# A hybrid retention and attention layer on one core: the feed forward in three chunks, with the output shares of two chunks computed as seven block products instead of eight

## The chip, the cores and the metric

The kernel runs on one core of a Trainium2 chip. The metric is the time of one execution on the device, in microseconds (us). The core's engines are named as in the profile: PE (matrix products; PEld is its loading of weights), DVE (vector engine), ACT (scalar engine), POOL and SP. SP issues nearly all DMA transfers here. The kernel is one hand-ordered program: each engine takes its instructions in the order in which the Python code emits them.

## The reference

One inference step of a layer, for a prompt of 512 tokens and for 8 sample tokens that continue from stored state. D_MODEL is 1024, the hidden width of the feed forward 2816 (22 x 128); all is fp32.

```python
proj = rmsnorm(x, g1) @ w_in            # q,k,v,g of 4 retention heads; q,k,v of 12 attention heads; 2 gates
o_r, s_new = retention(rotary(q_r), rotary(k_r), v_r, state, chunk=128)
branch_a = (group_norm(o_r) * gn_g * silu(g_r)) @ w_pa
branch_b = combine(dilated_attention(q_a, k_a, v_a)) @ w_pb      # three groups of heads
h = x + (sigmoid(gate_a) * branch_a + sigmoid(gate_b) * branch_b) @ w_o
a, b = split(rmsnorm(h, g2) @ w_ffn_in)
h = h + (silu(a) * b) @ w_ffn_out
y = rmsnorm(h, g_final)
```

Outputs are y, the retention states and the new keys and values, for prompt and samples.

## The kernel before

**Layout.** Activations lie transposed: 128 channels on the partitions, and on the free axis C = 520 columns in two halves f of HF = 260 (256 prompt tokens and 4 samples each). All weights of all projections lie in one tensor `wall` of 194 pieces ("subs") of 128x1024, in the order in which they are needed; a sub holds eight 128x128 tiles. A projection's output tile (128 channels) sums over its k-tiles: 8 where the input has 1024 channels, 22 for `w_ffn_out`.

**Products.** An fp32 product is made of three products of a shorter type (fp32r): both operands are split in a high part and the remainder, and w x = wh xh + wh xl + wl xh (`product`). With two halves, one tile of weights costs six matmuls of 128x260. `unit` runs `nk` tiles of weights into one buffer `pm` (two PSUM banks, one per half) and then calls the evacuation given to it.

**The weights' way.** SP loads a sub into one of four buffers `raw` (`load_sub`). `split_sub` has ACT copy it to `wh` (L153) and DVE subtract to `wl` (L157). At each eighth tile `unit` has the sub after next split; the subtraction and the next load are held back by two pumps:

```python
A.activation(h, r, AF.Copy)                                       # L153: wh
    V.tensor_tensor(l, r, f32(h), op=ALU.subtract)                # L157: wl
    load_sub(s + NRAW)
later(2, low)
```

**The order of the work.** After each tile of weights `unit` calls `pump`, which first runs what `later(n, ...)` held back for n pumps, and then lets the generators in the tracks P, S and Q go one step. So everything beside the big products (norms, attention, retention, the sample states) is emitted in steps between the matmuls. `drain` runs a track to its end at one place.

**The stages.** Norm and `w_in` with the retention heads (four of them, up to about 450 us), the gates, `w_pa`, attention, `w_pb`, `w_o`, then the feed forward. In a retention head, a generator updates the states of the 8 samples, two tiles of 128x512 each: ACT makes `kv` (L510) from `vb`, a broadcast load of one row (L502); DVE updates the state `st` (L545), SP stores it and reloads the buffer; ACT (L521) and DVE (L526) make `y` from it, and after each four samples PE sums four `y` into the bank `oacc` (L555). All this shares ACT and DVE with the splits of the weights.

**The feed forward.** It runs over 22 hidden tiles, each two units of eight k-tiles (a and b; `ev_fa`, `ev_fb` scale them by the norm `rs2`, L1112 multiplies them, ACT and DVE split the product into `U[i]` and `U[22 + i]`). Then come eight output tiles, each a unit of 22 k-tiles that `ev_f` adds to the residual `hT`. The last one is done a half at a time.

**The final norm.** For each output tile c and half f a round follows: `fin_T` transposes 2 x 128 tokens and 4 samples (three matmuls, L212) into two of the three side banks; `fin_sq` sums squares on ACT (L1142, L1144); `fin_g` multiplies by the gain on DVE (L1148, L1150) and so frees the banks. `gen_final(c)` emits both rounds of a tile in steps of the track P, beside the matmuls of the next tile. `fin_out(f)` ends a half: squares of tile 7, reduction (L1169), 1/rms (POOL), gain of tile 7, scaling, and the stores.

Of the kernel before, what the change touches and what calls it, by code (L numbers as in the profile page):

```python
# [23 lines left out]
NSUB = 194  # L24
GAMMA = [1.0 - 2.0 ** (-5.0 - h) for h in range(RH)]
# [3 lines left out]
def tile_hybrid_layer(  # L29
# [108 lines left out]
    raw, split = {}, {}  # L138

    NRAW = 4  # L140

    def load_sub(s):
# [4 lines left out]
    def split_sub(s):  # L147
        if s >= NSUB or s in split:
            return
        r = raw.pop(s)  # L150
        h = wpool.tile([128, 1024], F32R, tag="wh", name=f"wh{s}")
        l = wpool.tile([128, 1024], F32R, tag="wl", name=f"wl{s}")
        A.activation(h, r, AF.Copy)  # L153
        split[s] = (h, l)

        def low():
            V.tensor_tensor(l, r, f32(h), op=ALU.subtract)  # L157
            load_sub(s + NRAW)

        later(2, low)  # L160

# [20 lines left out]
    def product(pm, n, k, nk, src, fs):  # L182
        h, l = split[n // 8]
        j = n % 8
        wh, wl = h[:, j * 128:(j + 1) * 128], l[:, j * 128:(j + 1) * 128]
        xh, xl = src(k)
        for w, x, first, last in ((wh, xh, k == 0, False), (wh, xl, False, False), (wl, xh, False, k == nk - 1)):
            for f in fs:
                PE.matmul(pm[:, f, :HF], w, x[:, f * HF:(f + 1) * HF], start=first, stop=last)  # L189

    def unit(nk, src, evac=None):
        pm = pmain.tile([128, 2, 512], F32, tag="pm", name="pm")
        for k in range(nk):
            n = pos[0]
            pos[0] += 1
            if n % 8 == 0:
                for s in range(3):
                    split_sub(n // 8 + s)
# [4 lines left out]
        return pm[:, :, :HF]  # L203

# [42 lines left out]
    for s in range(2):  # L247
        split[s] = tuple(wpool.tile([128, 1024], F32R, tag=t, name=f"{t}{s}") for t in ("wh", "wl"))

    def w_split(s, i):  # L250
        q = slice(512 * i, 512 * i + 512)
        (h, l), r = split[s], raw[s]
        A.activation(h[:, q], r[:, q], AF.Copy)
        V.tensor_tensor(l[:, q], r[:, q], f32(h[:, q]), op=ALU.subtract)
# [10 lines left out]
    for s in range(2):  # L265
        raw.pop(s)
        load_sub(NRAW + s)
# [73 lines left out]
    for h in range(RH):  # L341
# [245 lines left out]
        for which in ("q", "k"):  # L587
            e0, e1 = rot(which)
            if h == 0 and which == "q":
# [3 lines left out]
                for u, k in [(u, k) for k in range(4) for u in range(2)] + [(u, k) for u in range(2) for k in range(4, 8)]:  # L593
                    product(pms[u], 8 * u + k, k, 8, src, (0, 1))
                    if u and k == 4:
                        split_sub(2)
# [446 lines left out]
    fp = open_pool("fp", "right")  # L1043
    X2 = bpool.tile([128, 16, C], F32R, tag="bx", name="X2")
# [50 lines left out]
    U = [None] * (2 * NFF)  # L1095
    UA = bpool.tile([128, 16, C], F32R, tag="bg", name="UA")
    UB = fp.tile([128, 28, C], F32R, name="UB")
    for i in range(2 * NFF):
        U[i] = UA[:, i, :] if i < 16 else UB[:, i - 16, :]
    for i in range(NFF):  # L1100
# [8 lines left out]
        def ev_fb(pm, i=i, s=s):  # L1109
            t = ftmp("fb")  # L1110
            V.tensor_tensor(halves(t), pm, halves(rs2), op=ALU.mult)  # L1111
            V.tensor_tensor(t, t, s["a"], op=ALU.mult)  # L1112
            A.activation(U[i], t, AF.Copy)
            later(2, lambda: V.tensor_tensor(U[NFF + i], t, f32(U[i]), op=ALU.subtract))
# [3 lines left out]
        if i == 0:  # L1118
            drain("P")
            ev_fa(pa)  # L1120
            ev_fb(pb)

# [29 lines left out]
    def gen_final(c):  # L1152
        for _ in range(5):
            yield
        a = fin_T(c, 0)
        yield
        fin_sq(c, 0, *a)
        fin_g(c, 0, *a)
        yield
        yield  # L1160
        b = fin_T(c, 1)
        yield
        fin_sq(c, 1, *b)
        fin_g(c, 1, *b)

    def fin_out(f, sp, sp2):
        fin_sq(7, f, sp, sp2)
# [3 lines left out]
        fin_g(7, f, sp, sp2)  # L1171
# [13 lines left out]
    def usrc(k):  # L1185
        return U[k], U[NFF + k]

    def ev_f(pm, c, f=None):
        fs = slice(None) if f is None else slice(f, f + 1)
        h = halves(hT[:, c, :])[:, fs]  # L1190
        V.tensor_tensor(h, pm[:, fs], h, op=ALU.add)
# [6 lines left out]
    for s in range(base // 8, NSUB):  # L1198
        split_sub(s)
    for f in range(2):  # L1200
        pm = pmain.tile([128, 2, 512], F32, tag="pm", name="pm")
        for k in range(NFF):
            product(pm, base + k, k, NFF, usrc, (f,))
            if f == 0 and k % 2:
                pump()
            if f == 1 and k == 2:
                a = fin_T(7, 0)
            if f == 1 and k == 5:
                fin_out(0, *a)
        ev_f(pm[:, :, :HF], 7, f)  # L1210
    a = fin_T(7, 1)
    fin_out(1, *a)
# [42 lines left out]
def _layout(np, i):  # L1255
# [9 lines left out]
    for h in range(AH):  # L1265
        for g in range(3):
# [3 lines left out]
    ffo = [j for c in range(NFF) for j in (c, NFF + c)]  # L1270
    flat = np.concatenate([x.reshape(-1, 128, 128) for x in
                           (w_in[seq], _tiles(f["w_pa"][0]), w_in[seq2], _tiles(f["w_pb"][0]), _tiles(f["w_o"][0]), ff[ffo],
                            _tiles(f["w_ffn_out"][0]))])
# [25 lines left out]
```

## Time and profile before

| | |
|---|---|
| Time, three runs | 1330.41, 1331.48 and 1332.78 us; median 1331.48 |
| The profiled execution | 1332.56 us, of it 1330.8 from its first to its last instruction (the span) |
| Mean granted clock of PE | 0.991 of full speed |
| After the last matmul of the products (L189) | 9.5 us |
| Moved from and to memory | 155.70 MB read, 25.98 MB written |

In the profile a line such as "L189 PE MATMUL pm<-X,wh" is a group of instructions: line of the kernel, engine, operation, output and inputs by the program's names. Behind it stand shape and count, the summed busy time in us and the mean of one in ns, and then the idle time in front of them on that engine, with what ended most of it. In the list of waits a row names who waited, for whom, the sum in us, the number of waits and the longest. The chain of waits is the work that ended last, followed back. A row of the chain in order of time starts with the moment and the duration, both in us. A window's row gives for a stretch the busy time of PE, PEld, DVE, ACT and POOL with the number of instructions, then the granted clock, the share of time of the DMA engines, and GB/s. In a row of the DMA view three numbers stand for a queue that waits for a transfer (sum, count, longest).

### The profile page before, as it was taken

The page shows a single profiled execution, that of the slowest core. Times are in us where ns is not written, and L with a number is a line of the kernel's source. Part 1 is how long each engine was busy: PE and PEld are TensorE (multiplying, and loading weights), DVE is VectorE, ACT ScalarE, POOL GpSimd, SP SyncE. Part 2 cuts the span into 40 slices and gives each one's busy share as a digit, 9 for nine tenths or more (in the row PEclk, how much of TensorE's full clock was granted, in tenths as well). Part 3 has the DMA queues.
Part 4 walks back from the last instruction along what each step waited for, and adds up shares of the span by engine and source line. Part 5 has one row for each costly group of instructions (what it writes and reads, how often), then busy time and mean ns, then how long its engine had stood idle before and what let it go on. Part 6 is the DMA issues. An engine that isn't in the chain of part 4 may idle for free.

```text
span 1330.8 us, 25131 instructions
## 1 busy us (share of the span) xinstructions
PE 1304.4 (98%) x10681; PEld 1273.4 (96%) x10681; DVE 662.5 (50%) x1271; ACT 476.7 (36%) x828; POOL 83.0 (6%) x69
## 2 busy tenths in 40 slices
PE   8999999999989999999999999999999999999997
PEld 7899999898889999999999999899999999999997
DVE  7867536746655432233545454376444444443323
ACT  4554334534453421143434343233222222222222
POOL 3601001001002000000000000030000000000000
PEclk9999999999899999999999999999999999999999
DMA  6267235646475233435555455634223332333221
GB/s 216 84 227 231 89 114 206 228 129 230 157 255 189 80 96 95 135 115 160 156 159 164 134 171 175 217 104 136 82 94 96 96 90 86 95 112 96 80 64 66
DMA packets 89777, 183.33 MB, mean 138 GB/s; under 512 B 12024, under 2 KB 33944, under 8 KB 89664
## 3 DMA queue, kind: packets, MB, share of 16 engines
q1 hardware_dynamic: 88944, 180.64, 43.2%
q8 instruction: 84, 1.38, 0.4%
q10 hardware_dynamic: 720, 1.07, 0.2%
q14 instruction: 29, 0.24, 0.1%
HBM read 155.70 MB, written 25.98 MB: 137 GB/s over the span
## 4 chain that ended last, share of the span: by engine, by line
PE 89%; DVE 4%; DMA 3%; ACT 1%; issue 1%; POOL 1%; SPq 1%; POOLq 0%; DVEq 0%; ACTq 0%
PE pm L189 78%; PE sp L212 3%; PE sp L442 2%; DMA vb<-vd 2%; PE sp L460 2%; DVE wl L157 1%; PE sp L394 1%; PE sp L852 1%; PE sp L802 1%; PE oacc L555 1%; PE sacc L997 1%; PE sp L791 0%; ACT wh L153 0%; DMA xb<-xT 0%; DVE X L313 0%
## 5 line engine op out<-in xcount | busy, mean ns | idle before, releaser
L189 PE MATMUL pm<-X,wh 128*128 128x260 f32 x4608 | 756.6, 286 | 3.9 <-DVE X L244 3.6
L189 PEld LDWEIGHTS pm<-X,wh 128*128 128x128 f32 x4608 | 636.7, 189 | 19.3 <-issue 8.2
L189 PE MATMUL pm<-X,wl 128*128 128x260 f32 x2304 | 465.0, 283 | 0.0
L189 PEld LDWEIGHTS pm<-X,wl 128*128 128x128 f32 x2304 | 356.3, 189 | 0.1
L157 DVE TENSOR_TENSOR wl<-raw,wh 128x1024 fp32r<-128x1024 f32 x192 | 236.6, 1233 | 169.9 <-ACT wh L153 169.2
L153 ACT ACTIVATE wh<-raw 128x1024 fp32r<-128x1024 f32 x192 | 201.7, 1051 | 174.2 <-PE pm L189 169.0
L189 PE MATMUL pm<-UB,wh 128*128 128x260 f32 x448 | 85.3, 282 | 0.0
L189 PE MATMUL pm<-GA,wh 128*128 128x260 f32 x512 | 82.2, 283 | 0.0
L189 PEld LDWEIGHTS pm<-GA,wh 128*128 128x128 f32 x512 | 70.1, 188 | 0.0
L189 PEld LDWEIGHTS pm<-UB,wh 128*128 128x128 f32 x448 | 67.2, 188 | 0.0
L221 POOL TENSOR_TENSOR r<-v,cst 128x4 f32<-128x4 f32 (+4 forms) x14 | 18.4, 1313 | 609.9 <-DVE v L219 609.8
L189 PE MATMUL pm<-UA,wh 128*128 128x260 f32 x256 | 55.3, 287 | 0.0
L510 ACT ACTIVATE kv<-vb,ks 128x512 f32<-128x512 f32 x64 | 44.0, 715 | 29.8 <-DMA vb<-vd 29.8
L545 DVE SCALAR_TENSOR_TENSOR st<-st,kv 128x512 f32<-128x512 f32 x64 | 45.9, 733 | 16.7 <-ACT kv L510 16.7
L189 PE MATMUL pm<-UA,wl 128*128 128x260 f32 x256 | 54.2, 283 | 0.0
L189 PE MATMUL pm<-GA,wl 128*128 128x260 f32 x256 | 51.6, 283 | 0.0
L1106 ACT ACTIVATE fa<-fa 128x520 f32<-128x520 f32 x22 | 14.0, 638 | 78.4 <-DVE fa L1105 78.4
L189 PE MATMUL pm<-M,wh 128*128 128x260 f32 x256 | 41.1, 282 | 0.0
L189 PEld LDWEIGHTS pm<-UA,wh 128*128 128x128 f32 x256 | 40.4, 188 | 0.3
L189 PEld LDWEIGHTS pm<-UA,wl 128*128 128x128 f32 x256 | 40.5, 188 | 0.0
L189 PEld LDWEIGHTS pm<-GA,wl 128*128 128x128 f32 x256 | 39.6, 188 | 0.0
L1111 DVE TENSOR_TENSOR fb<-pm,rs 128x520 f32<-128x520 f32 x22 | 15.4, 700 | 46.2 <-PE pm L189 46.2
(245 smaller groups left out, 1309.7 us busy)
## 6 DMA issues: line engine op xcount, KB each, us to landing
raw<-wall SPq DMA_DIRECT2D x192, 512.0 KB
st<-state SPq DMA_DIRECT2D x64, 256.0 KB
out<-st SPq DMA_DIRECT2D x64, 256.0 KB
area<-ck SPq DMA_DIRECT2D x24, 512.0 KB
vb<-vd SPq DMA_DIRECT2D x32, 256.0 KB
area<-qd SPq DMA_DIRECT2D x12, 512.0 KB
cb<-cd SPq DMA_DIRECT2D x4, 768.0 KB
xr<-xT SPq DMA_DIRECT2D x8, 260.0 KB
```

The source lines that it names most:

```text
L153: A.activation(h, r, AF.Copy)
L157: V.tensor_tensor(l, r, f32(h), op=ALU.subtract)
L189: PE.matmul(pm[:, f, :HF], w, x[:, f * HF:(f + 1) * HF], start=first, stop=last)
L212: PE.transpose(out, in_, ident[:n, :n])
L221: G_.tensor_tensor(r[:rows, :ncol], v[:rows, :ncol], mhalf[:rows].to_broadcast([rows, ncol]), op=ALU.pow)
L394: PE.matmul(sp[:, :T - i0], x[:, dt, jb * 128:(jb + 1) * 128], y[:, dt, i0:], start=i == 0, stop=i == len(mm) - 1)
L442: PE.matmul(sp[:, i0:], v[x][:, jb, c * 128:(c + 1) * 128], scs[y][:, SCO[jb]:SCO[jb] + T - i0], start=jb == 0 and x == y, stop=jb == 3 an ...
L460: PE.matmul(sp, kt[x][:, jb, dt * 128:(dt + 1) * 128], v[y][:, jb, :], start=jb == 0 and x == y, stop=jb == 3 and x == 1)
L510: A.activation(kvs[i][:, :DV], vbs[b], AF.Copy, scale=ks[:, dt, b:b + 1])
L545: V.scalar_tensor_tensor(sts[i], sts[i], GAMMA[h], kvs.pop(i)[:, :DV], op0=ALU.mult, op1=ALU.add)
L1106: A.activation(t, t, AF.Silu)
L1111: V.tensor_tensor(halves(t), pm, halves(rs2), op=ALU.mult)
```

## The change

**Blocks of 512.** Weights are split in blocks of 512 columns instead of 1024. `wh` and `wl` have six buffers of 512 each, and `advance` keeps the copies five blocks ahead of the product that runs. A `raw` buffer is reloaded when its second half is subtracted.

**Three chunks.** The hidden tiles are cut in chunks of 8, 8 and 6. After each of the first two chunks (and one tile of the next) comes that chunk's share of all eight output tiles, added to `hT`. The hidden tiles of the first two chunks are kept as `UF`, four blocks per pair of k-tiles: even or odd k-tile, half 0 or 1.

**Seven products.** `quad` computes two output tiles c, c+1 over eight k-tiles. The weights form a 2x2 block matrix A (rows: the two output tiles; columns: the even and the odd k-tiles), the activations a 2x2 block matrix B (rows: even and odd k-tiles; columns: the halves). The product of the two is made of seven block products instead of eight. Their left sides are A11, A21+A22, A11+A21+A22, A12, A11+A21, the sum of all four, and A22; their right sides are B11, B21, B22 and four differences, which `right` computes once per pair of k-tiles (DVE), copies to `UH` (ACT) and splits to `UL` (DVE). Each block product has 4 tiles x 3 matmuls of 260 columns, all into one bank. ACT copies four partial sums out of the banks while they go on being summed (L290), and DVE adds the seven results into `hT` in five operations of 260 columns and one of 520 (L1241 to L1249). There are four pairs of output tiles in each of two chunks, eight `quad`s.

**Sums of weights.** Of the four sums on the left, A21+A22 and A11+A21 are made by DMA: SP loads A21 twice into a buffer `qq` (a broadcast load of 512 KB, L167), and POOL's queue adds [A22, A11] to it with an accumulating DMA of 512 KB (L169). The other two are each one addition of 128x512 on DVE (`block_sum`).

**The last chunk and the end.** Output tiles 0 and 1 run interleaved over its six k-tiles, tiles 2 and 3 as units; tiles 4 to 7 run for half 0, then for half 1. `gen_final(c, fs)` takes the halves that are ready. The queue P of final rounds is drained at one place in half 1, ahead of `fin_out(0)`, and once more after the last matmul.

```diff
     def load_sub(s):
         if s < NSUB:
             raw[s] = wpool.tile([128, 1024], F32, tag="raw", bufs=NRAW, name=f"raw{s}")
             SP.dma_start(raw[s], wall[s])
+        if s - 1 in QUADS:
+            w = 128 * QUADS[s - 1]
+            q = qsum[s - 1] = home[0].tile([128, 1024], F32, tag="qq", bufs=2, name=f"qq{s}")
+            SP.dma_start(q[:, :2 * w].rearrange("p (i c) -> p i c", i=2),
+                         wall[s, :, :w][:, None, :].to_broadcast([128, 2, w]))
+            G_.dma_start(q[:, :2 * w], wall[s - 1, :, :2 * w], accum_op=ALU.add)
...
+        t, i = ((s, 1), ("q", 0), (s + 1, 0), (s + 1, 1), ("q", 1), ("q", 0), (s, 0))[j]
+        return (qsum[s] if t == "q" else raw[t])[:, i * w:(i + 1) * w]
...
+        if j == 2:
+            V.tensor_tensor(raw[s + 1][:, :w], raw[s][:, w:2 * w], qsum[s][:, :w], op=ALU.add)
+        elif j == 5:
+            V.tensor_tensor(qsum[s][:, :w], raw[s + 1][:, w:2 * w], raw[s + 1][:, :w], op=ALU.add)
...
+    def block_hi(b):
+        h, l = block_tiles(b)
+        r = left(b)
         A.activation(h, r, AF.Copy)
...
             V.tensor_tensor(l, r, f32(h), op=ALU.subtract)
-            load_sub(s + NRAW)
+            kind, s, j = blocks[b]
+            if kind == "p" and j == 1:
+                load_sub(s + NRAW)
+            elif kind == "q" and j == 6:
+                load_sub(s + NRAW)
+                load_sub(s + 1 + NRAW)
         later(2, low)
+    def advance(t):
+        while done["add"] < min(t + AHEAD + 2, len(blocks)):
...
+            block_sum(b)
+        while done["hi"] < min(t + AHEAD + 1, len(blocks)):
...
+            block_hi(b)
...
+    SEVEN = ((0, 0), (1, 3), (0, 4), (2, 1), (0, 5), (1, 2), (0, 6))
+    def quad(xh, xl, snap, evac):
...
+        for j, (bank, x) in enumerate(SEVEN):
+            advance(bid[s, 0] + j)
...
+                for w, r in ((h, xh), (h, xl), (l, xh)):
+                    PE.matmul(out[bank], w[:, ks], r[:, k, x, :], ...)
...
+                if k % 2:
+                    pump()
+            if j in (0, 1, 2, 4):
+                A.activation(snap[(0, 3, 1, None, 2)[j]], out[bank], AF.Copy)
+            evac(j, out[bank])
+    def right(t, hi, lo):
+        V.tensor_tensor(t[:, 3, :], t[:, 0, :], t[:, 7, :], op=ALU.subtract)
+        V.scalar_tensor_tensor(t[:, 4, :], t[:, 2, :], -1.0, t[:, 3, :], op0=ALU.mult, op1=ALU.subtract)
+        V.tensor_tensor(t[:, 5, :], t[:, 2, :], t[:, 7, :], op=ALU.subtract)
+        V.scalar_tensor_tensor(t[:, 6, :], t[:, 4, :], -1.0, t[:, 1, :], op0=ALU.mult, op1=ALU.subtract)
+        A.activation(hi, t[:, 0:7, :], AF.Copy)
+        later(3, lambda: V.tensor_tensor(lo, t[:, 0:7, :], f32(hi), op=ALU.subtract))
...
+    for (a, n), ahead in zip(CHUNKS, (1, 1, 0)):
+        if not ahead:
+            whole(NP, UF[:, 0::7, :])
+        for i in range(a and a + 1, a + n + ahead):
+            ffn_in(i)
+        if ahead:
+            for c in range(0, 8, 2):
+                ffn_out(c)
...
-    for c in range(7):
-        unit(NFF, usrc, lambda pm, c=c: ev_f(pm, c))
-        push("P", gen_final(c))
...
+    for c in (2, 3):
+        unit(nk, usrc, lambda pm, c=c: ev_f(pm, c))
         push("P", gen_final(c))
...
     for f in range(2):
+        for c in range(4, 8):
...
+            for k in range(nk):
...
+                if k % 2:
+                    pump()
+                if f and c == 4 and k == 3:
+                    a = fin_T(7, 0)
+                if f and c == 4 and k == 5:
+                    fin_sq(7, 0, *a)
+                    fin_g(7, 0, *a)
+                if f and c == 5 and k == 1:
+                    drain("P")
+                    fin_out(0)
+            ev_f(o[:, :, :HF], c, f)
+            if c < 7:
+                push("P", gen_final(c, (f,)))
+    drain("P")
     a = fin_T(7, 1)
-    fin_out(1, *a)
+    fin_sq(7, 1, *a)
+    fin_g(7, 1, *a)
+    fin_out(1)
```

In all, PE has 10585 matmuls instead of 10681. The line numbers of the new kernel are higher: L153 is L197 there, L157 is L200, L212 is L309, L545 is L641, L526 is L622.

**PE near the end.** Before, the transposes of the final rounds (two of 128x128 into one side bank, one of 4x128 into another) stand between matmuls of the products, a round at a time; the names `sp_...` are side banks, `pm_...` the output banks:

```order
L212 MATMUL sp_14451<-cst_90,hT_9984 128x128 x2
L212 MATMUL sp_14452<-cst_90,hT_9984 4x128
L189 MATMUL pm_14441<-UA_10510,wh191_14200 128x260
L189 MATMUL pm_14441<-UB_10511,wh191_14200 128x260
L189 MATMUL pm_14441<-UA_10510,wl191_14201 128x260
```

The round here is followed at once by a product of tile 7 (`pm_14441`).

With the change seven rounds follow each other at the place of the first `drain`; the last matmul ahead of them and the first three:

```order
L1356 MATMUL pm_15244<-UH_11030,wl407_14993 128x260
L309 MATMUL sp_15296<-cst_90,hT_10472 128x128 x2
L309 MATMUL sp_15297<-cst_90,hT_10472 4x128
L309 MATMUL sp_15309<-cst_90,hT_10472 128x128 x2
L309 MATMUL sp_15310<-cst_90,hT_10472 4x128
L309 MATMUL sp_15322<-cst_90,hT_10472 128x128 x2
L309 MATMUL sp_15323<-cst_90,hT_10472 4x128
```

Behind the seventh come 48 matmuls of the products, with one more round among them, and after the last matmul two rounds.

**SP at the first group of pairs.** Before, the loads of the weights stand one after another (`raw148` is the load of sub 148):

```order
L145 DMA raw148_11382<-wall 128x1024
L145 DMA raw149_11440<-wall 128x1024
L145 DMA raw150_11500<-wall 128x1024
L145 DMA raw151_11558<-wall 128x1024
L145 DMA raw152_11618<-wall 128x1024
```

Nothing else lies between them.

With the change each pair has a load into `qq` behind its two subs (here the pairs at 148 and 150):

```order
L162 DMA raw148_11966<-wall 128x1024
L162 DMA raw149_12028<-wall 128x1024
L167 DMA qq149_12030<-wall 128x2x512
L162 DMA raw150_12240<-wall 128x1024
L162 DMA raw151_12242<-wall 128x1024
L167 DMA qq151_12244<-wall 128x2x512
```

So SP's queue has three loads per pair, and POOL's has one accumulating DMA into each `qq` behind them. With four `raw` and two `qq` buffers, the loads of a pair are issued when the last half tile of the pair two places earlier has been subtracted.

**DVE in a pair and in a retention head.** In a pair (subs 150 and 151 here) the additions of weights (L185; the other, L187, follows below), the subtractions of the half tiles and the additions into `hT` take turns:

```order
L200 TENSOR_TENSOR wl306_12384<-raw150_12240,wh306_12383 128x512
L185 TENSOR_TENSOR raw151_12242<-raw150_12240,qq151_12244 128x512
L200 TENSOR_TENSOR wl307_12402<-qq151_12244,wh307_12401 128x512
L1241 TENSOR_TENSOR hT_10472<-pc_12404,hT_10472 128x260
L1242 TENSOR_TENSOR hT_10472<-hT_10472,s12_12339 128x520
L200 TENSOR_TENSOR wl308_12420<-raw151_12242,wh308_12419 128x512
L1244 TENSOR_TENSOR s35_12340<-s35_12340 128x260
L200 TENSOR_TENSOR wl309_12438<-raw151_12242,wh309_12437 128x512
L1246 TENSOR_TENSOR hT_10472<-pm_12341,hT_10472 128x260
L1247 TENSOR_TENSOR hT_10472<-hT_10472,s35_12340 128x260
```

These rows are new; before, DVE had one subtraction (L157) per sub and the evacuation of each output tile here.

In a retention head before, the subtraction of a whole sub (L157) stands ahead of the state update (L545) and of the `y` (L526) made from it:

```order
L157 TENSOR_TENSOR wl49_4419<-raw49_4100,wh49_4418 128x1024
L545 SCALAR_TENSOR_TENSOR st_4236<-st_4236,kv_4413 128x512
L526 SCALAR_TENSOR_TENSOR y_4427<-st_4236,qs_3544,y_4427 128x512
L639 COPY gs_4165<-g_4164 128x8
L545 SCALAR_TENSOR_TENSOR st_4409<-st_4409,kv_4442 128x512
```

With the change, around the same `y` (L622):

```order
L200 TENSOR_TENSOR wl99_4615<-raw49_4280,wh99_4614 128x512
L641 SCALAR_TENSOR_TENSOR st_4423<-st_4423,kv_4609 128x512
L622 SCALAR_TENSOR_TENSOR y_4623<-st_4423,qs_3704,y_4623 128x512
L200 TENSOR_TENSOR wl100_4660<-raw50_4367,wh100_4659 128x512
L735 COPY gs_4349<-g_4348 128x8
L641 SCALAR_TENSOR_TENSOR st_4605<-st_4605,kv_4638 128x512
```

Ahead of the update and the `y` now stands only the second half of sub 49 (`wl99`; the first was subtracted five rows earlier), and behind it the first half of sub 50.

More of the change, by code (lines that the diff above doesn't have):

```diff
@@ L135, in finish @@
             step(name)
-    raw, split = {}, {}
+    raw, split, qsum = {}, {}, {}
+    blocks, bid = [], {}
+    for s_ in range(NSUB):
+        if s_ in QUADS:
+            bid[s_, 0] = len(blocks)
+            blocks += [("q", s_, j) for j in range(7)]
+        elif s_ - 1 not in QUADS:
+            bid[s_, 0], bid[s_, 1] = len(blocks), len(blocks) + 1
+            blocks += [("p", s_, 0), ("p", s_, 1)]
+    done = {"add": 0, "hi": 0}
+    home = []
     NRAW = 4
+    AHEAD = 5
     def load_sub(s):
@@ L203, in unit @@
         return pm[:, :, :HF]
+    SEVEN = ((0, 0), (1, 3), (0, 4), (2, 1), (0, 5), (1, 2), (0, 6))
+    def quad(xh, xl, snap, evac):
+        s = pos[0] // 8
+        pos[0] += 16
+        nkp = QUADS[s]
+        pm = pmain.tile([128, 2, 512], F32, tag="pm", name="pm")
+        out = [pm[:, 0, :HF], pm[:, 1, :HF], None]
+        begun = set()
+        for j, (bank, x) in enumerate(SEVEN):
+            advance(bid[s, 0] + j)
+            if bank == 2:
+                out[2] = abank("pc")[:, :HF]
+            h, l = split[bid[s, 0] + j]
+            for k in range(nkp):
+                ks = slice(k * 128, k * 128 + 128)
+                for w, r in ((h, xh), (h, xl), (l, xh)):
+                    PE.matmul(out[bank], w[:, ks], r[:, k, x, :], start=bank not in begun, stop=k == nkp - 1 and r is xh and w is l,
+                              skip_group_check=True)
+                    begun.add(bank)
+                if k % 2:
[10 more added lines that the diff above has]
+        later(3, lambda: V.tensor_tensor(lo, t[:, 0:7, :], f32(hi), op=ALU.subtract))
     def sbank(name="sp"):
@@ L245, in x0_split @@
                                op1=ALU.subtract)
-    for s in range(2):
-        split[s] = tuple(wpool.tile([128, 1024], F32R, tag=t, name=f"{t}{s}") for t in ("wh", "wl"))
+    for b in range(4):
+        block_tiles(b)
+    done["add"] = done["hi"] = 4
     def w_split(s, i):
[L251 to L254, printed above, removed]
+        (h, l), r = split[2 * s + i], left(2 * s + i)
+        A.activation(h, r, AF.Copy)
+        V.tensor_tensor(l, r, f32(h), op=ALU.subtract)
     for i in range(2):
@@ L265, in tile_hybrid_layer @@
     for s in range(2):
-        raw.pop(s)
         load_sub(NRAW + s)
@@ L1094, in tile_hybrid_layer, with whole, ffn_in @@
     push("P", gen_norm2())
[L1095 to L1100, printed above, removed]
+    UH = bpool.tile([128, 28, HF], F32R, tag="bg", name="UH")
+    UL = fp.tile([128, 28, HF], F32R, name="UL")
+    UF = fp.tile([128, 8, HF], F32, name="UF")
+    UH4, UL4 = (u.rearrange("p (k x) c -> p k x c", x=7) for u in (UH, UL))
+    UHp, ULp = (u.rearrange("p (k f) c -> p k (f c)", f=2) for u in (UH, UL))
+    NP = CHUNKS[2][0]
+    def whole(i, t):
+        hi, lo = (halves(u[:, i - NP, :]) for u in (UHp, ULp))
+        A.activation(hi, t, AF.Copy)
+        later(2, lambda: V.tensor_tensor(lo, t, f32(hi), op=ALU.subtract))
+    def ffn_in(i):
         s = {}
@@ L1190, in ev_f @@
         h = halves(hT[:, c, :])[:, fs]
-        V.tensor_tensor(h, pm[:, fs], h, op=ALU.add)
+        V.tensor_tensor(h, pm, h, op=ALU.add)
     pattern[:] = ["P"]
-    for c in range(7):
-        unit(NFF, usrc, lambda pm, c=c: ev_f(pm, c))
+    nk = CHUNKS[2][1]
+    pms = [pmain.tile([128, 2, 512], F32, tag="pm", name="pm") for _ in range(2)]
+    base = pos[0]
+    for i, (c, k) in enumerate(LAST):
+        begin(base + i)
+        product(pms[c], base + i, k, nk, usrc, (0, 1))
+        pump()
+        if k == nk - 1:
+            ev_f(pms[c][:, :, :HF], c)
+            push("P", gen_final(c))
```

138 lines of the change are left out of this document (91 added, 47 removed).

## The prediction

> **What bounds the kernel now.** I read the page's first and fourth parts, then the chain of waits in order of time.
>
> ```profile
> span 1330.8 us, 25131 instructions
> PE 1304.4 (98%) x10681; PEld 1273.4 (96%) x10681; DVE 662.5 (50%) x1271; ACT 476.7 (36%) x828; POOL 83.0 (6%) x69
> ...
> 946.10 263.93 PE pm L189 x2196
> ...
> 1314.47 6.85 PE pm L189 x57
> ```
>
> PE is busy 98% and the chain is mostly PE's own matmuls. The two chain rows give the price of one: 263.93 / 2196 = 0.120 us where two halves alternate between banks, and 6.85 / 57 = 0.120 us at the end, where every matmul goes to one bank. So in the feed forward a matmul of 260 columns costs 0.120 us whichever bank it goes to. What hides beside it:
>
> ```profile
> 1000.00:1100.00 100.00, 100.00 (x835) 100.00 (x834) 45.19 (x53) 27.90 (x36) 0.00 (x0) 1.00 0.32 94
> ```
>
> In this stretch of the feed forward (columns: PE, PEld, DVE, ACT, POOL, clock, DMA share, GB/s) DVE is 45% busy, ACT 28%, the DMA engines 32%. Outside it, PE waits almost only in the retention stage:
>
> ```profile
> PE oacc L555 <- DVE y L526: 4.9, 2, 3.4
> ...
> PE sp L394 <- DVE pl L382: 2.2, 2, 1.2
> ...
> PE sp L394 <- DVE ph L382: 1.5, 1, 1.5
> ```
>
> Two of these stalls cost more than their length, because the granted clock falls behind them (windows of the same columns):
>
> ```profile
> 324.80:328.20 3.40, 2.34 (x13) 1.51 (x14) 1.35 (x3) 0.59 (x1) 0.00 (x0) 1.00 0.75 231
> 331.40:334.80 3.40, 1.20 (x7) 0.68 (x6) 3.29 (x4) 2.85 (x4) 0.00 (x0) 1.00 0.95 320
> 334.80:341.60 6.80, 5.55 (x16) 4.67 (x17) 4.64 (x7) 3.30 (x5) 0.00 (x0) 0.50 0.97 315
> 389.40:392.90 3.50, 1.37 (x10) 0.32 (x8) 2.32 (x4) 2.91 (x5) 0.00 (x0) 0.99 0.95 293
> 392.90:399.70 6.80, 5.53 (x16) 3.58 (x17) 4.34 (x7) 3.59 (x6) 0.00 (x0) 0.51 0.84 258
> ```
>
> PE busy 1.20 of 3.40 us, or 1.37 of 3.50, is followed by 6.8 us at half clock; 2.34 of 3.40 is not.
>
> **1. The products removed: -11.5 us.** A pair of output tiles over eight k-tiles took 2 x 8 x 2 halves x 3 = 96 matmuls; seven block products over four k-tiles are 7 x 4 x 3 = 84. Eight pairs make 96 fewer, 96 x 0.120 = 11.5. The row at 1314.47 excludes a penalty for staying in one bank.
>
> **2. Halves of 512 instead of 1024 for every weight.**
>
> ```profile
> L157 DVE TENSOR_TENSOR wl<-raw,wh 128x1024 fp32r<-128x1024 f32 x192 | 236.6, 1233 | 169.9 <-ACT wh L153 169.2 <-DMA xr<-xT 0.8
> L153 ACT ACTIVATE wh<-raw 128x1024 fp32r<-128x1024 f32 x192 | 201.7, 1051 | 174.2 <-PE pm L189 169.0 <-issue 5.0 <-DMA raw<-wall 0.2
> ...
> L253 ACT ACTIVATE wh<-raw x4: 613/624/634, 4.5 to 10.9; 128x512 fp32r<-128x512 f32 x4
> L254 DVE TENSOR_TENSOR wl<-raw,wh x4: 685/1240/1805, 5.3 to 15.4; 128x512 fp32r<-128x512 f32 x4
> ```
>
> Two 512-wide ones cost 2 x 0.624 - 1.051 = 0.20 us more on ACT and, by the shortest of L254 (its median lies beside POOL's work), 2 x 0.685 - 1.233 = 0.14 on DVE: some 38 and 27 us over the kernel, hidden under PE as the window at 1000 shows; uncovered, up to 27 would be paid. The gain is that less stands in front of what PE waits for. Before the 3.40 us stall:
>
> ```profile
> 390.35 1.04 ACT L153 ACTIVATE wh<-raw 128x1024 fp32r<-128x1024 f32 x1
> ...
> 391.42 1.22 DVE L157 TENSOR_TENSOR wl<-raw,wh 128x1024 fp32r<-128x1024 f32 x1 [0.77 <-ACT wh L153]
> 392.56 0.68 DVE L545 SCALAR_TENSOR_TENSOR st<-st,kv 128x512 f32<-128x512 f32 x1
> ...
> 393.36 0.75 DVE L526 SCALAR_TENSOR_TENSOR y<-st,qs,y 128x512 f32<-128x512 f32 x1
> ```
>
> PE waits for that y; wh and wl stand in its way, and in the new order one 512-wide half stands there: 0.42 + 0.54 = 1.0 us less. The other oacc wait and the L394 waits each have one wl ahead of them: 0.5 each. I take -2.0 and leave the clock as it is. Bounds: +4 (nothing gained, and one more spell of 6.8 us at half clock, worth 3.4) to -9 (both spells gone as well). Raw loads stay in SP's order; ACT waited 0.2 us for them in all, and needs them half a piece earlier.
>
> **3. The accumulating DMA: +0.5 us.** Each pair adds a 512 KB broadcast load on SP and a 512 KB accumulating one on POOL's queue, which no run here shows.
>
> ```profile
> raw<-wall SPq DMA_DIRECT2D x192, 512.0 KB
> ...
> vb<-vd SPq DMA_DIRECT2D x32, 256.0 KB
> ...
> SPq L764 <- DMA qd<-qr: 36.0, 12, 6.4
> ...
> 379.22 5.98 DMA vb<-vd
> ```
>
> 94 GB/s at a share of 0.32 is 294 GB/s, so 512 KB (524 kB) moves in 1.8 us; a 4 KB DMA (qd) keeps SP waiting 36.0 / 12 = 3.0 us. An accumulate then takes 4.8 us if the add is free and 6.6 if its target is read at the same price; the far bound is the 256 KB load in the chain, 5.98 us, so 12 for 512 KB. The tight places are the third pair of each group of four. Its loads are issued when the first pair's last half-tile is split, about 3.4 us after that pair starts (one block of 12 matmuls 1.44, ACT's copy 0.46, its split 0.62, DVE's 0.69, hand-overs); three loads of 1.8 and 3.0 land the broadcast at 11.8, the accumulate at 16.6 to 18.4. The first sum on DVE and a split on ACT want it 10 blocks after that start, at 14.4. They wait, and behind them stand DVE's evacuation of the pair that is running and ACT's copy of its partial sum, which PE needs before block 13, at 18.7; two splits and that copy earlier is 17.0. So PE loses up to 1.4 per group; the fourth pair only inherits the delay, and nothing else stands on POOL's queue until the end. I take 0.5 in all (the plain load and the small DMA are the nearest rows), bounds 0 and 2 x 6.8 = 13.6. By the Trainium skill, "DMA: Bandwidth & Descriptors" (Anatomy of one DMA), 2.0 us plus bytes at 436 GB/s, this transfer would be an estimated 3.2 us; "Collectives: The Full Stack" (The bandwidth ceiling) holds that an add halves the rate by its second read, so 4.4: the term would be 0. No run here shows either.
>
> What the two engines do in a pair, 84 x 0.120 = 10.1 us of PE:
>
> ```profile
> L1148 DVE TENSOR_TENSOR yt<-sp,gb 128x256 f32<-128x256 f32 x16 | 6.8, 424 | 25.3 <-ACT junk L1142 25.3
> ...
> L414 ACT ACTIVATE kth<-sp,cst 128x256 fp32r<-128x256 f32 x16 | 6.5, 464 | 0.3 <-PE sp L212 0.3
> ...
> L1112 DVE TENSOR_TENSOR fb<-fb,fa 128x520 f32<-128x520 f32 x22 | 15.4, 700 | 0.8
> ```
>
> DVE: 9 halves and sums x 0.69, five of 260 columns at about 0.42, one of 520 at 0.70, together 9.0 us. ACT: 7 x 0.62 and four copies of 0.46, 6.2. Full on DVE, but it fits, and its halves are due four blocks later, so I cost it nothing; a tenth more per operation would still be 9.9. Between the pairs each two hidden tiles add on DVE four operations of 260 columns and widen one subtraction to 1820, some 2.5 us more per 23, beside a PE that DVE follows at 45%: nothing too.
>
> **4. The end: +7.9 us.** The final stage queues its 16 transpose-and-square rounds one step per pump, and has fewer pumps than steps; the rest is emptied at one place, with 48 matmuls left: seven rounds in a row on PE. One round before:
>
> ```profile
> 1294.66 0.49 PE L212 MATMUL sp<-cst,hT 128*128 128x128 f32 x3
> ...
> 1294.91 0.48 PE L189 MATMUL pm<-UA,wh 128*128 128x260 f32 x2
> ...
> 1295.14 0.28 ACT L1142 ACTIVATE junk<-sp 128x128 f32<-128x128 f32 x1 [1.62 <-PE sp L212]
> ...
> 1295.80 0.42 DVE L1148 TENSOR_TENSOR yt<-sp,gb 128x256 f32<-128x256 f32 x1 [1.87 <-ACT junk L1142]
> 1295.82 0.18 ACT L1144 ACTIVATION_READ_ACCUMULATOR junk<-sp 4x1 f32 x1
> ...
> 1296.14 0.27 DVE L1150 TENSOR_TENSOR ys<-sp,gb 4x128 f32<-4x128 f32 x1
> ```
>
> A round takes PE 1294.91 - 1294.66 = 0.25 us and holds two of three side banks until DVE has read them, 1.75 us after its start (1296.41); ACT works 1296.00 - 1295.14 = 0.86 in it. PE can therefore run ahead by no more than a round and a half, and seven in a row go at ACT's pace, which I put at 0.93 with the hand-overs: PE gets past the last after 0.5 + 6 x 0.93 = 6.1 us, of which 7 x 0.25 are transposes that it ran anyway, so **+4.4** (bounds 3.4 at 0.86 flat, 8.8 where rounds don't overlap at all). Behind the rounds on DVE stand the evacuations of the last columns, which nothing on PE waits for until the next round. In such a stretch PE is busy 0.49 of each 0.93 us, 53%, between the 35% that lost the clock and the 69% that kept it; I take it as lost, with some 5 of the 6.8 us falling on the 48 matmuls: **+2.5** (0 to 3.4). The Trainium skill, "TensorE: Matmul & The Clock Gate" (Part 1), has free-running windows of 3.4 us and half clock after an idle one, which the rows at 331 and 389 bear out, and says in Part 4 that transposes hardly count as busy; by it the 2.5 would be sure.
>
> ```profile
> 1321.03 0.28 PE L189 MATMUL pm<-UB,wl 128*128 128x260 f32 x1
> ...
> 1322.37 0.28 ACT L1142 ACTIVATE junk<-sp 128x128 f32<-128x128 f32 x1 [4.71 <-PE sp L212]
> ...
> 1323.02 0.17 DVE L1169 TENSOR_REDUCE fs<-ssp 128x2 f32<-128x16 f32 x1 [1.25 <-ACT junk L1142]
> ...
> 1323.31 0.42 DVE L1148 TENSOR_TENSOR yt<-sp,gb 128x256 f32<-128x256 f32 x1
> ```
>
> After the last matmul another round (c = 6) now goes first, and the reduction stands behind the two products of c = 7: 0.3 + 0.7 = **+1.0**.
>
> **Sum.** -11.5 - 2.0 + 0.5 + 4.4 + 2.5 + 1.0 = -5.1. The profiled execution took 1332.56 (span 1330.8), 1.08 above the median; so 1327.5 for it, and 1326.4 for the median of 1331.48.
>
> **The rivals.**
> *The end costs next to nothing* (PE runs ahead of ACT, clock kept): 1326.4 - 6.9 = 1319.5. For: ACT is nearly idle there. Against: the three banks.
> *The accumulating DMA becomes the bound of the pairs*, the slower side: at 12 us PE loses 6.8 in each group, 1326.4 - 0.5 + 13.6 = 1339.5. It decides from about 9.3 us per accumulate, where 2 x 4.1 eats the gain and 0.2% more. For: every pair needs it and no row prices the add. Against: 4.8 to 6.6 by the plain rows.
> *The retention stage goes another way*: both half-clock spells gone, 1326.4 - 6.8 = 1319.6; or no gain and one more, 1326.4 + 5.4 = 1331.8. In the window rows PE's 1.37 us of 3.50 lost the clock and 2.34 of 3.40 kept it: about 1 us of PE's work more or less in one of these tips it.
>
> **How the numbers follow.** Forecast 0.50 (of it 0.42 faster, 0.08 same, as the end may cost up to 4 more); cheap end 0.17, faster; spells gone 0.07, faster; retention worse 0.12 (0.08 same, 0.04 slower); DMA late 0.14 (0.03 same, 0.11 slower). Faster by over 0.2% (under 1328.8; this kernel's runs cannot tell less from no change): 0.66, within 0.2% 0.19, slower (over 1334.1) 0.15. The range, 1317 to 1335, leaves out the late DMA's upper part and a cheap end together with lost spells; the forecast's own is 1322 to 1330.
>
> **What would show it.** PE instructions 10585. Between the first pair and the last, matmuls 0.120 us apart, and no wait of PE on a copy or on DMA in the third pair of a group. About 4.4 us of waits on side banks near the end, then a granted clock of 0.5. An oacc wait of some 2.4 instead of 3.40 us. I am wrong if the pairs show waits on qq, if DVE is late with wl there, or if the seven rounds cost under 2 us.

## The result, and the profile after

The changed kernel takes 1347.12 us (median; 1345.44 to 1349.92) beside 1331.24 for the kernel before. The ratio is 1.012, 95% interval 1.0099 to 1.0141: **slower by 1.2%**. Forecast were 1326.4 and a range of 1317 to 1335. The profiled execution took 1345.44, with a span of 1343.7, 12.9 more than the 1330.8 before. The sums below are made against these two spans.

The head of the page after:

```profile
span 1343.7 us, 25725 instructions
PE 1301.0 (97%) x10585; PEld 1261.4 (94%) x10585; DVE 748.3 (56%) x1578; ACT 535.3 (40%) x1068; POOL 90.8 (7%) x77
```

PE has the 96 matmuls less that were forecast. It is busy 3.4 us less than before, and the span is longer, so PE waits more. Its waits in the kernel after (us in total, times, longest):

```profile
PE pm L284 <- ACT s L290: 11.4, 24, 0.5
PE pm L284 <- DVE hT L1246: 4.2, 8, 0.5
...
PE sp L309 <- DVE yt L1287: 2.8, 7, 0.9
...
PE oacc L651 <- DVE y L622: 1.6, 2, 1.2
...
PE pm L1356 <- DVE hT L1325: 1.5, 4, 0.6
```

L284 is the matmul of the seven products, L290 ACT's copy of a partial sum, L1246 DVE's addition of a result into `hT`. L1287 is DVE's product with the gain in a final round, L1325 the addition of an output tile or half tile into `hT` at the end. 24 and 8 waits are 32, four in each of the eight pairs. One of them in order of time (first two columns: start and duration):

```profile
1032.83 0.28 PE L284 MATMUL pm<-UH,wl 128*128 128x260 f32 x1
...
1033.15 0.39 ACT L290 ACTIVATE s<-pm 128x260 f32<-128x260 f32 x1 [0.60 <-PE pm L284]
...
1033.59 0.38 PE L284 MATMUL pm<-UH,wh 128*128 128x260 f32 x1 [0.48 <-ACT s L290]
```

The last matmul of the first block product starts at 1032.83. ACT copies its bank from 1033.15 to 1033.54. The first matmul of the second block product starts at 1033.59, 0.05 after the copy's end. But that matmul writes the *other* bank. From start to start it is 0.76 us instead of 0.120.

In every pair the last matmul starts some 12.96 us after the first, where 83 x 0.120 = 9.96 were to be expected. The extra 3.0 us lie at the starts of blocks 2, 3, 6 and 7, four times some 0.65 and 0.10 at the matmul after each. Eight pairs: **24.0 us**. The window of a group of four pairs (columns as in the windows of before):

```profile
1031.40:1083.80 52.40, 44.60 (x339) 41.27 (x338) 34.57 (x61) 22.09 (x44) 1.76 (x2) 1.00 0.50 139
```

PE is busy 44.60 of 52.40 us at full clock. DVE with 34.57 and ACT with 22.09 are not full.

The whole difference of the spans, worked out from the start of the last matmul of piece 145 (the same 7008 products stand before it in both kernels; 1039.65 before, 1031.40 after) and of the last matmul of all:

| | us |
|---|---|
| up to the first pair | -8.25 |
| 96 matmuls fewer | -11.5 |
| waits in the eight pairs | +24.0 |
| the rest up to the last matmul, mostly the end | +8.6 |
| after the last matmul | +0.1 |
| sum | +12.9 |

### The profile page after: what moved, and what is told of

It reads as the page before. It is cut to its first block, busy times and chain, and to the rows that moved or that the text cites. A ratio compares the mean times of both kernels' runs of the same rounds, so it can differ in the third digit from the quotient of the medians.

```text
span 1343.7 us, 25725 instructions
## 1 busy us (share of the span) xinstructions
PE 1301.0 (97%) x10585; PEld 1261.4 (94%) x10585; DVE 748.3 (56%) x1578; ACT 535.3 (40%) x1068; POOL 90.8 (7%) x77
## 4 chain that ended last, share of the span: by engine, by line
PE 89%; DVE 4%; DMA 2%; ACT 2%; issue 1%; POOL 1%; SPq 0%; DVEq 0%; ACTq 0%
PE pm L247 70%; PE pm L284 6%; PE sp L309 2%; DMA vb<-vd 2%; PE sp L538 2%; PE sp L556 2%; PE pm L1356 1%; PE sp L948 1%; PE sp L490 1%; PE pc L284 1%; ACT s L290 1%; DVE wl L200 1%; PE sp L898 1%; PE sacc L1093 1%; DVE X L409 0%
## 5 line engine op out<-in xcount | busy, mean ns | idle before, releaser
L200 DVE TENSOR_TENSOR wl<-raw,wh 128x512 fp32r<-128x512 f32 x384 | 275.0, 720 | 225.4 <-ACT wh L197 222.9
L197 ACT ACTIVATE wh<-raw 128x512 fp32r<-128x512 f32 x384 | 237.8, 625 | 241.9 <-PE pm L247 181.8
L284 PE MATMUL pm<-UH,wh 128*128 128x260 f32 x192 | 57.6, 300 | 15.6 <-ACT s L290 11.4
L284 PEld LDWEIGHTS pm<-UH,wh 128*128 128x128 f32 x192 | 36.1, 188 | 22.3 <-ACT s L290 16.4
L284 PE MATMUL pm<-UL,wh 128*128 128x260 f32 x192 | 54.2, 282 | 0.0
L284 PE MATMUL pm<-UH,wl 128*128 128x260 f32 x192 | 54.1, 282 | 0.0
L641 DVE SCALAR_TENSOR_TENSOR st<-st,kv 128x512 f32<-128x512 f32 x64 | 45.3, 712 | 11.8 <-ACT kv L606 11.7
L284 PEld LDWEIGHTS pm<-UL,wh 128*128 128x128 f32 x192 | 36.1, 188 | 0.0
L284 PEld LDWEIGHTS pm<-UH,wl 128*128 128x128 f32 x192 | 36.1, 188 | 0.0
L866 DVE SCALAR_TENSOR_TENSOR area<-area 128x128 f32<-128x128 f32 x96 | 22.7, 287 | 22.8 <-DMA area<-qd 20.9
```

What stands on the lines that cost most here:

```text
L284: PE.matmul(out[bank], w[:, ks], r[:, k, x, :], start=bank not in begun, stop=k == nkp - 1 and r is xh and w is l, skip_group_check=True)
L641: V.scalar_tensor_tensor(sts[i], sts[i], GAMMA[h], kvs.pop(i)[:, :DV], op0=ALU.mult, op1=ALU.add)
L866: V.scalar_tensor_tensor(pr[:, e], kb[:, e], 1.0, qb[:, e], op0=ALU.mult, op1=ALU.mult, accum_out=Ss[:, g, 32 * h + b:32 * h + b + 1])
```

## The experiments

The theory, W: PE waits because both output banks of a pair are one buffer `pm` of two banks. The program's waits are set for a buffer as a whole, so whoever reads one bank holds up the writer of the other. The rival, P: the engines lack room in a pair, or reading a bank holds up PE in its neighbour.

### The two banks in two buffers

```diff
-        pm = pmain.tile([128, 2, 512], F32, tag="pm", name="pm")
-        out = [pm[:, 0, :HF], pm[:, 1, :HF], None]
+        two = [pmain.tile([128, 2, 512], F32, tag="pm", name="pm") for _ in range(2)]
+        if s // 2 % 2 == 0:
+            two.reverse()
+        out = [two[0][:, 0, :HF], two[1][:, 0, :HF], None]
```

> The changed kernel with one edit: the two output banks of a pair of tiles lie in two different output buffers (the first bank of each) instead of the two banks of one buffer, and the next pair takes them in the other order. Theory W (the loss is PE waiting, at four of the seven block starts of each pair, for ACT's copy or DVE's addition that reads the other bank of the same buffer, 0.63 us each, because a buffer is waited for as a whole): the four waits go, a pair takes 84 x 0.120 = 10.1 us instead of 13.1, 8 x 3.0 = 24 us less, so 1347.1 - 24 = 1323. Rival P (ACT and DVE have no room in a pair, or reading a bank holds up PE in the neighbouring one): pairs stay above 12 us and the time above 1339. Rival D (only half of it: DVE, 9.0 us busy in 10.1, becomes the bound once the waits are gone): pairs near 11.5, about 1334, with waits of PE on wl or on additions into hT.

Measured: 1327.31 (ratio to before 0.9968, 0.9954 to 0.9981), 19.8 less than the changed kernel, where 24 were expected. The matmuls, copies and additions are the same; only where the second bank lies is changed. ACT's copies in the second pair, with PE beside them:

```profile
1045.38 0.28 PE L286 MATMUL pm<-UL,wh 128*128 128x260 f32 x1
...
1045.46 0.39 ACT L292 ACTIVATE s<-pm 128x260 f32<-128x260 f32 x1 [0.67 <-PE pm L286]
...
1045.50 0.28 PE L286 MATMUL pm<-UH,wl 128*128 128x260 f32 x1
...
1045.62 0.28 PE L286 MATMUL pm<-UH,wh 128*128 128x260 f32 x1
```

PE writes one bank at 0.120 us a matmul while ACT reads another. The pairs take 10.1 to 10.6 us, but for the last two of the second group. So W holds, and the engines had room. The instruction listing says the same. In the changed kernel the seventh block's first matmul waits for DVE's addition out of the other bank; with the banks apart it waits for an ACT copy out of its own bank, made two blocks earlier:

```
changed:     L284 MATMUL pm_12206<-UH_11030,wh298_12224 128x260 [waits DVE_49]
banks apart: L286 MATMUL pm_12206<-UH_11030,wh298_12225 128x260 [waits Activation_49]
```

Likewise the second block's first matmul waits in the changed kernel for ACT's copy out of the first bank, and with the banks apart only for ACT's copy of its own weights. So the waits stand in the program, and PE starts 0.05 us after they end. The other half of P, that reading a bank holds up PE in its neighbour, isn't tested by this run: the two banks used here, 0 and 2, are no neighbours. In the kernel before, though, the two buffers `pm` are banks 0 and 1 and banks 2 and 3, and PE kept its 0.120 us over 2196 matmuls while DVE read whole buffers beside it. Whether two banks of one two-bank buffer could be read and written at once without the wait wasn't tried. The PE waits of this run show where the rest of the 24 went:

```profile
PE pm L286 <- ACT s L292: 2.7, 1, 2.7
```

One long wait is left, in the third pair of the second group; that pair took 14.2 us. (The profiled execution, 1330.87, was the slowest of the ten, so this stall may be longer than usual.) The chain of waits there:

```profile
1188.63 9.02 DMA qq<-wall
1197.64 0.02 issue
1197.67 0.70 DVE raw L185
...
1198.53 0.10 ACT wh L197
...
1199.07 0.38 ACT s L292
...
1199.48 0.59 PE pm L286
```

The accumulating DMA took 9.0 us, DVE's sum waited for it, ACT's copy of the weights for that sum, ACT's copy of the partial sum stood behind it, and PE waited. 6.8 us at half clock followed, from 1198.8. This is the path that the prediction named for the third pair of a group, but the transfer here holds the sums of the fourth pair, for which DVE waits while the third runs. (The expectation of the next run calls it the third pair's.) In the first group it was the third pair's: it landed at 1050.09, DVE's sum waited 1.6 us for it, and PE lost some 1.2 us, 0.6 ahead of the third pair and 0.5 in it. In the changed kernel, with pairs of 13.1 us, PE has no wait behind these transfers.

### The weight sums earlier, and without DMA

The loads into `qq` six pieces earlier, four buffers:

```diff
-        if s - 1 in QUADS:
+        if s in EARLY:      # {140: 146, 141: 148, 142: 150, 143: 152, 164: 170, ...}
+            p = EARLY[s]
...
-            q = qsum[s - 1] = home[0].tile([128, 1024], F32, tag="qq", bufs=2, name=f"qq{s}")
+            q = qsum[p] = home[0].tile([128, 1024], F32, tag="qq", bufs=4, name=f"qq{p + 1}")
```

> The kernel with the output banks apart, and the broadcast load and the accumulating DMA of a group's four pairs issued six pieces earlier, into four buffers instead of two. With the banks apart, the accumulating DMA of the third pair of the second group took 9.0 us there and held up DVE's sum, ACT's copies behind it and PE, 4.1 us and then half clock; the third of the first group cost 0.5. Theory A (that lateness is why the step gave 20 instead of 24): all eight pairs take 10.1 to 10.4 us, no wait on the sums, time 1331.8 - 7.4 (blocks) - 11.5 (fewer matmuls) + 9 (the end) = 1322. Rival D (DVE, 9.0 busy of 10.1, is what is late there): pairs keep 10.6 or more in places and the time 1326 or 1327.

And the banks apart, with DVE making those two sums instead:

```diff
+        if j == 1:
+            for i in range(2):
+                V.tensor_tensor(qsum[s][:, i * w:(i + 1) * w], raw[s][:, i * w:(i + 1) * w], raw[s + 1][:, :w], op=ALU.add)
```

> The kernel with the output banks apart, and the two sums of weights that DMA made computed by DVE (two more additions of 128x512 per pair, no load into qq, no accumulating DMA). Theory: DVE then has 9.0 + 1.4 = 10.4 us of work in a pair of 10.1 and becomes its bound; pairs of 10.4 to 10.9, 8 x 0.5 = 4 above the kernel with early sums, so 1326, but without the 4.1 us stall. Rival: DVE has slack from the hidden tiles between the groups, and four pairs are too few to use it up: 1322, no different from early sums.

Measured: 1323.92 with early sums (ratio 0.9936, 0.992 to 0.9953) and 1323.65 with the sums on DVE (0.9931, 0.9916 to 0.9946). In both, the first pair of a group takes 10.3 to 10.4 us and the other six 10.09. Three pairs of each, early sums first:

```profile
1045.40:1075.70 30.30, 30.30 (x255) 30.30 (x254) 24.18 (x45) 16.59 (x33) 0.00 (x0) 1.00 0.40 122
```

```profile
1044.30:1074.60 30.30, 30.30 (x255) 30.30 (x254) 26.07 (x49) 16.58 (x33) 0.00 (x0) 1.00 0.40 124
```

PE is busy all the time in both. DVE has 24.18 / 3 = 8.1 us of work in a pair, and 26.07 / 3 = 8.7 with the sums. So theory A holds, and for the sums on DVE the theory fell and the rival came true: DVE does not become the bound. My 9.0 added up mean durations of instructions, and those overlap: in the kernel after, two 260-wide DVE operations of 0.43 and 0.42 us start 0.35 apart. The accumulating DMA brings nothing here that DVE could not have done in its idle time.

### Blocks of 512 alone, and their halves at one place

The kernel before, with the splits in blocks of 512 and nothing else:

```diff
-            if n % 8 == 0:
-                for s in range(3):
-                    split_sub(n // 8 + s)
+            begin(n)        # if n % 4 == 0: advance(block), five blocks ahead
```

> The kernel before with the splits in blocks of 512 alone, feed forward and end as before. Theory S (the 8.2 us that the changed kernel is ahead by the time of its first pair come from the shorter pieces: the spells of half clock at 17, 335 and 393 us shortened or gone, and shorter waits): 1331.2 - 8 = 1323, with half clock only in one spell of 3.4 us before the feed forward. Rival: they come from something else in the changed kernel or from chance between executions: 1331, the spells back.

Both halves where the whole piece was:

```diff
-        if n % 4 == 0:
+        if n % 8 == 0:
             advance(bid[n // 8, n % 8 // 4])
```

> As the one before, blocks of 512, but both halves of a piece are copied and subtracted at the place where the whole piece was in the kernel before. Theory S (what counts is how much stands in one lump ahead of the retention work): nearly nothing is left of the gain, 1330 to 1332. Rival H (two instructions instead of one help by themselves, since the subtraction of the first half starts before the copy of the second ends): most of the gain stays, 1323 to 1326.

Measured: 1324.37 (ratio 0.994, 0.9923 to 0.9958) for the blocks alone, 1330.56 (0.9987, 0.9977 to 0.9996) for the halves together. The waits for `y` in the two, blocks alone first:

```profile
PE oacc L610 <- DVE y L581: 1.7, 2, 1.3
```

```profile
PE oacc L610 <- DVE y L581: 4.5, 2, 2.8
```

Before it was 4.9, the longest 3.4. The spell of 6.8 us at half clock behind it is gone with halves apart, the one at 335 us is down to 3.4. With both halves at one place a spell of 3.4 us stays at 393, one of 6.8 at 335, and nearly all of the gain is gone. So the size of the lump ahead of the retention work is what counts, not the number of instructions: theory S holds.

### Eight products in the same chunks

```diff
-QUADS = {s + 2 * i: 4 for s in (146, 170) for i in range(4)}
+QUADS = {}
...
+    def ffn_out(c, a):
+        for d in range(2):
...
+            unit(8, lambda k: usrc(k, a), ev)
```

> The changed kernel (blocks of 512, three chunks, its end) with the shares of the first two chunks computed as plain units of eight k-tiles, eight block products and no sums of weights; 10681 matmuls again. Theory W: no waits between the shares, since each unit has a buffer of its own, so this is the kernel before less 8.2 for the blocks plus 8.5 for the end: 1331.5, i.e. 15.6 faster than the changed kernel and 11.5 - 3 slower than nothing else but the end would make it. Rival: cutting the feed forward in chunks costs by itself (evacuations of sixteen more units): 1335 or more.

Measured: 1334.62 (ratio 1.002, 1.001 to 1.0031). Beside the blocks alone, 1324.37, this prices the chunks and the new end at 10.2 us in the medians; the spans of the two profiled executions, 1330.4 and 1322.3, differ by 8.1. The shares of the first group run without a gap:

```profile
1031.20:1077.30 46.10, 46.10 (x387) 46.10 (x386) 17.25 (x26) 10.67 (x17) 0.00 (x0) 1.00 0.29 94
```

So the chunks as such cost nothing there, and from 1031 to 1230 us no matmul of the products starts late; it is the end. The median is 3.1 us above what was expected and only 0.4 below the rival's 1335. The trace, of the fastest of the ten executions (1332.22), speaks against the rival's reason, but what makes up the 3.1 us isn't shown. With early sums the seven products take 1334.62 - 1323.92 = 10.7 us less than the eight, and 11.6 less when each is set against the runs of the kernel before that were taken with it (1331.80 and 1332.66): the gain forecast at 11.5 is real once PE waits for nobody.

### The end

Each half tile of the end in a buffer of its own, on top of early sums:

```diff
-            if c % 2 == 0:
-                pm = pmain.tile([128, 2, 512], F32, tag="pm", name="pm")
-            o = pm[:, c % 2:c % 2 + 1, :]
+            pm = pmain.tile([128, 2, 512], F32, tag="pm", name="pm")
+            o = pm[:, 0:1, :]
```

> The kernel with early sums, and at the end each half tile in a buffer of its own instead of two of them in the two banks of one. Theory W (a buffer is waited for as a whole): the four waits of PE on the evacuation L1325, some 0.65 us each, go: 2.6 less, 1319.5 if early sums give 1322. Rival: they only move into the burst of final rounds: no difference.

Measured: 1321.4 (ratio 0.9916, 0.9901 to 0.9931), 2.5 less. The four waits on the addition (L1325 in the changed kernel) are gone, and from piece 145 to the end of the span it is 289.4 us before this edit and 287.2 after it. W again.

Then the final rounds paced, each in one side bank:

```diff
-        sp, sp2 = sbank(), sbank()
+        sp = sbank()
+        sp2 = sp[:, 256:384]
...
-                    drain("P")
-                    fin_out(0)
...
+                beat(1)      # one round at most per four beats, as soon as its half tile is there
```

> The one before, and the final rounds spread over the last three stretches, one every 12 matmuls at most and each in one side bank instead of two, none drained at one place. Theory (the burst costs 4.4 and the half clock behind it 1.7): 6 less, 1313.5, no half clock before the last matmul. Rival (ACT or DVE can't follow at that pace, the waits spread as well): 1317 or more.

Measured: 1321.15 (ratio 0.9921, 0.9905 to 0.9938): the medians show no gain, where 6 us were expected. (From piece 145 to the end of the span the trace has 285.5 us.) Half clock before the last matmul is gone, but the waits on the side banks have turned into others:

```profile
PE sp L312 <- DVE hT L1346: 4.0, 4, 2.6
```

The longest stands at 1297.3. DVE is scaling half 0 there and waits for POOL's 1/rms, and the next addition into `hT`, which the next transposes need, stands behind it. So this wait was taken out:

```diff
-                fin_out(0)
+                rr = fin_stat(0)         # reduction and 1/rms
             yield
             yield
+            if (c, f) == (5, 1):
+                fin_scale(0, *rr)        # scaling and stores
```

> The kernel with the paced rounds, with the last scaling of half 0 moved behind the round of tile 5, half 1, and in the last round the reduction ahead of the gain products. With paced rounds PE had one wait left of 2.7 us (a start to the next start of 2.84) in the end: DVE's additions into hT stood behind the scaling, which waits for POOL's 1/rms. Theory D (DVE's order there is what kept the pacing from giving its 6 us): that wait goes, 2.7 less, and 0.5 less at the very end: 1321.2 - 3 = 1318. Rival (pacing has no more to give, the wait moves to the next addition): 1320 to 1322.

Measured: 1317.83 (1316.88 to 1319.83; ratio 0.9899, 0.988 to 0.9918):

```profile
PE sp L312 <- DVE hT L1351: 3.3, 5, 1.4
```

At the old place PE now waits 0.4 us instead of 2.6. But the scaling, moved behind the round of tile 5, holds up another addition there, and that gives the longest wait, 1.4:

```profile
1301.94 0.86 DVE L1340 TENSOR_SCALAR yt<-yt,r 128x512 f32<-128x512 f32 x2
1302.73 0.73 DVE L1342 TENSOR_SCALAR ys<-ys,r 4x1024 f32<-4x1024 f32 x1
1303.39 0.41 DVE L1351 TENSOR_TENSOR hT<-pm,hT 128x260 f32<-128x260 f32 x1
```

So theory D holds for the wait that it named, and the rival for half of it: the wait moved. From piece 145 to the end of the span it is 284.0 us after this edit, 1.5 less than before it, half of it behind the last matmul. The medians differ by 3.3, but they were taken beside different runs of the kernel before (1332.66 and 1331.10), and the intervals of the two ratios overlap, so a gain of 3 us is not shown. This version beats both kernels, before by 1.0% and the changed one by 29 us.

## Why the prediction was wrong

**The step that failed** is the one on ACT and DVE in a pair: "Full on DVE, but it fits, and its halves are due four blocks later, so I cost it nothing", and with it "ACT's copy of its partial sum, which PE needs before block 13". I let PE need a copy only when it comes back to the copied bank, one block product later. The runs showed that it needs each read of either bank to be over before the next block product into the same buffer. That is four waits a pair and 24.0 us. The change's code had it: both banks are slices of one `pm`. The kernel before never writes one bank of a buffer while the other is read, so its trace had no row that showed it. I asked whether the work fits, and not who waits at each block start. The Trainium skill, "Perfetto Trace Analysis" (Matmuls), advises rotating matmul groups through PSUM banks so that evacuations overlap. By this case that holds between buffers (0.120 us a matmul beside ACT's copy with the banks apart) and not between two banks of one buffer with the waits of this program.

By terms, forecast and measured in the profiled executions:

- **The products removed: -11.5.** Right. A pair that waits for nobody takes 10.09 us, 84 x 0.120; seven products instead of eight are worth 10.7 to 11.6 in the medians.
- **Halves of 512: -2.0 (+4 to -9).** Measured -8.25, near the far bound. The wait fell as forecast and further: 3.40 us before, forecast some 2.4, found 1.2. (The waits that the term names add up to 1.0 and four times 0.5, 3.0, and not to 2.0.) To "leave the clock as it is" was the miss. Half clock up to the feed forward came down from 17.0 us to 3.4, worth 6.8; of it the spell at 17 us, worth 1.7, comes and goes between executions, as the last section shows. The rival "both half-clock spells gone" came nearly true (0.07). The blocks alone gave 7.4 in the medians.
- **The accumulating DMA: +0.5.** In the changed kernel PE waited for none of it, and its pairs were slower than the term assumed; 5.2 to 6.1 us from issue to landing, inside the 4.8 to 6.6 that I had worked out and above the estimates of 3.2 and 4.4 that stood beside the term:

```profile
DMA to landing us min/median/max: 5.2/5.5/6.1
```

  With the banks apart the path was real. In the first group the third pair's transfer landed 16.6 us after the group's start (forecast 16.6 to 18.4) and cost some 1.2 us. In the second group the fourth pair's, of which I had said that it "only inherits the delay", took 9.0 us and cost some 4 in the third pair, with more half clock behind it. The 9.0 came near the rival's 9.3 and did not reach it.
- **The end: +6.9 up to the last matmul.** Measured 8.6. The burst was right; its windows, with the spell behind it:

```profile
1319.70:1326.10 6.40, 4.13 (x24) 2.07 (x23) 3.76 (x12) 5.77 (x40) 0.00 (x0) 1.00 0.00 0
1326.10:1329.50 3.40, 3.40 (x18) 3.40 (x17) 2.52 (x10) 1.75 (x6) 1.26 (x2) 0.50 0.06 19
```

  ACT is busy 5.77 of 6.40 us. From 1319.77 to 1326.06 it is 6.3 us, forecast 6.1. The half clock came, for 3.4 us and not for 5 (1.7 instead of 2.5). That is this execution's: at the same burst with early sums it lasted 6.8 us (1303.4 to 1310.2). The rest is the four waits on L1325, the same whole-buffer wait a second time, some 0.65 from start to start each, which I had not seen either.
- **After the last matmul: +1.0.** Measured 0.1.

Forecast -5.1, measured +12.9. The 18.0 between them are 24.0 of waits, -6.25 on the blocks, -0.5 on the DMA, +1.7 on the end and -0.9 after it. The rivals had the slower side by the wrong mechanism: I gave 0.11 to a late DMA that makes it slower, 0.04 to the retention stage, and nothing to a wait on the banks inside the pairs.

## What to carry to other kernels

Where a change lets one engine read a bank that is still being summed, ask at every block start which reads have to be over, and of which buffer, not which bank; two banks in one buffer were one thing to the waits of this program. A wait that returns in each of many short steps (some 0.75 us with what follows it, 32 times) can outweigh the whole arithmetic gain (11.5 us here), and hide other lateness until it is removed. Where a trace shows a clock lost behind a stall, splitting the lump in front of the stall can be worth more than the stall itself: the waits for `y` fell by 3.2 us, the time by 7.4.

## What the runs showed of the hardware

An accumulating DMA of 512 KB took 5.2 to 6.1 us from issue to landing in the changed kernel; 5.4 to 9.0 with the banks apart, where the pairs ran at full speed; and 7.1 to 9.9 with early sums:

```profile
DMA to landing us min/median/max: 7.1/7.8/9.9
```

The spells of half clock differ between executions of the same instructions. Up to piece 124 the kernels with the banks apart, with early sums and with paced rounds have the instructions of the changed kernel. The changed kernel ran at full clock at 17 us, the one with early sums at half clock, and their lead over the kernel before was 8.2 and 4.75 us at piece 124. The windows, the changed kernel first:

```profile
16.60:23.40 6.80, 6.13 (x51) 6.13 (x52) 5.76 (x9) 2.35 (x4) 0.00 (x0) 1.00 0.47 131
332.80:336.20 3.40, 3.40 (x14) 3.28 (x13) 2.07 (x4) 1.19 (x3) 0.00 (x0) 0.50 0.93 305
```

```profile
16.60:23.40 6.80, 6.06 (x28) 6.06 (x29) 4.21 (x8) 1.86 (x4) 0.00 (x0) 0.50 0.38 125
334.00:340.80 6.80, 6.14 (x21) 5.75 (x22) 4.59 (x8) 2.84 (x6) 0.00 (x0) 0.50 0.86 325
```

So up to 3.5 us of a difference between two single executions here comes with the clock. Comparisons of a few microseconds are safer between medians, or between stretches that have the same clock.
